# Moving constants and raw weight tiles to the lower end of SBUF, and six weight units to the upper end, in a two-layer hybrid decoder trunk

## The chip, the cores and the metric

The kernel runs on one core of a Trainium2 chip. The metric is the device time of one execution in microseconds (us). One execution was also profiled; its trace is what the views below are taken from.

## The reference

Input x is (1, 1024, 1024) float32: 1024 positions, 1024 features. Two layers follow each other, each a token mixer and a dense feed-forward part, both with a residual addition and an RMS norm ahead of them; a last RMS norm closes the trunk.

```python
for layer in range(2):
    hn = rms_norm(h, norm_mix_g[layer])
    if layer % 2 == 0:
        h = h + mixer_ab(hn, ...)     # gated DeltaNet heads, short gated convolutions
    else:
        h = h + mixer_cd(hn, ...)     # HGRN2 heads, dilated sliding-window attention
    hn = rms_norm(h, norm_ffn_g[layer])
    h = h + (silu(hn @ w_gate[layer]) * (hn @ w_up[layer])) @ w_down[layer]
return rms_norm(h, norm_final_g)
```

The feed-forward width is 2816, which is 22 blocks of 128.

## The kernel before

**Numbers.** Every large product is made in float32r with both operands split into a high and a low part. `split` (L103, L104) lets ScalarE copy the float32 source into the high part and VectorE subtract to get the low part. `mm3` (L127 to L129) then issues three matmuls for each block: high weights with high data, high weights with low data, low weights with high data. Each has a 128x128 stationary block (the weights) and a moving tile of 128x512; in two functions of the second mixer, `swa_v` and `hgrn_v`, the sides are exchanged: the normalised data hn is stationary and a 128x256 piece of weights moves. In all, `mm3` issues 3750 such triples.

**SBUF.** Tiles come from pools that are stacked from either end of SBUF, the lower ("left") or the upper ("right"). Three are open throughout: "hnp" at the lower end with eight quarters (8192 bytes per partition each) for the normalised data; "ring" at the upper end with four weight units `w` (8192 bytes: a high and a low half), two raw tiles (4096 bytes) into which DMAs bring weights, and a pad; and "const", below the ring, with masks, the identity, gains and a pad. All others are opened and closed stage by stage between these. A tile that takes the place of an earlier one waits for that tile's last users.

**Weights.** For every product the SP queue loads a raw tile from DRAM (L116 in the mixers, L267 in the gate and up projections, L518 in the down projection), and the splits turn it into a unit. TensorE waits for a unit's two halves only.

**Gate and up projections (class `Up`).** For each f of the 22 blocks the gate and up products are combined by a Strassen-Winograd scheme of seven half-size products on both 512-position halves at once: a11, a12, s1, s2, s3, a22 and s4, 12 matmuls each. Their moving tiles are quarters: two of the norm (hn in the trace), t1 and b22 in hnp, t2, t3 and t4 in the pool "hx". Four weight units are filled for each f, by four calls of `part`: part_a (a11 and a12), part_b (s2 and s1), part_c (s3 and a22), part_d (s4). GpSimd makes the sums that b, c and d need. `part` counts its calls, and from the ninth on, two of every six take a unit in the pool "up" (tags w0 and w1), the other four one of the ring:

```python
self.n += 1
i = self.n - 9
u = self.right.tile([P, 2, DM], F32R, tag=f"w{i % 6}", name="w", bufs=1) if i >= 0 and i % 6 < 2 else unit()
```

From f = 3 on this puts parts c and d on w0 and w1 where f is a multiple of 3, parts a and b where f leaves 2, and none where f leaves 1. Together with part d of f = 1 and part b of f = 2, 576 matmuls of each layer have their weights there. The pool "up" lies directly below const and also holds four tiles `hid` for results on their way to DRAM and four tiles `kr` for kept partial sums. In `end`, the a22 and s4 products of one f close its two results, which VectorE (L370) and GpSimd (L378) multiply and the SP queue stores.

**Down projection (`down`).** Products over all 22 blocks, with the hidden values loaded back from DRAM, split into hidq tiles, and weights through raw tiles and ring units. Before the results are added to the residual (L537), h is loaded back from DRAM (L168) into tiles of the pool "trunk", which take the place of what "up" held.

**Order.** The start of `Up` (`turn`) is issued in the written order on TensorE, VectorE, ScalarE and GpSimd; elsewhere a scheduler orders each engine's instructions when the program is built.

Addresses in the program as built, in bytes within a partition:

| tiles | before | after |
|---|---|---|
| const | 183296 to 188288 | 16512 to 21504 |
| raw (two) | 221056 to 229248 | 21504 to 29696 |
| hn quarters (hnp) | 16512 + 8192 n | 29696 + 8192 n |
| t2, t3, t4 (hx) | 82048 + 8192 n | 95232 + 8192 n |
| w0, w1 (up) | 150528, 175104 | 180096, 188288 |
| four ring units | 188288 + 8192 n | 196480 + 8192 n |
| hid (four) | 158720 to 166912 | 163712 to 171904 |
| kr (four) | 166912 to 175104 | 171904 to 180096 |

Of the kernel before, what the change touches and what calls it, by code (L numbers as in the profile page):

```python
# [9 lines left out]
F32 = mybir.dt.float32  # L10
# [8 lines left out]
P = 128  # L19
T_LEN = 1024  # L20
DM = 1024
# [31 lines left out]
def hybrid_trunk_kernel(ctx: ExitStack, tc: tile.TileContext, x_t, w_all, w_four, w_down, w_ba, vecs, c_f, c_i, c_rope, out):  # L53
# [4 lines left out]
    def pool(name, side="left", space=None):  # L58
        kw = {} if space is None else {"space": space}
        if space is None:  # L60
            kw["side"] = side
        if space is not DRAM:
            kw["reuse_waits"] = "tile"
        return tc.tile_pool(name=name, bufs=1, **kw)

    hnp = ctx.enter_context(pool("hnp"))
    ring = ctx.enter_context(pool("ring", side="right"))
    const = ctx.enter_context(pool("const", side="right"))
    ps = ctx.enter_context(pool("ps", space=PSUM))
    dr = ctx.enter_context(pool("dr", space=DRAM))  # L70

# [19 lines left out]
    def psg():  # L91
        return ps.tile([P, HT], F32, tag="g", name="psg", bufs=2)
# [4 lines left out]
    def psm():  # L97
        return ps.tile([P, HT], F32, tag="m", name="psm", bufs=3)


    def split(hi, lo, src, eng=V):

        S.copy(hi, src)  # L103
        eng.tensor_tensor(lo, src, hi.bitcast(F32), op=SUB)  # L104

    def unit():

        return ring.tile([P, 2, DM], F32R, tag="w", name="w", bufs=4)

    def wload(*names):  # L110

        us = []
        for n in names:
            us.append(unit())
            raw = ring.tile([P, DM], F32, tag="raw", name="raw", bufs=2)
            dma(raw, w_all[W_AT[n]])  # L116
            split(us[-1][:, 0, :], us[-1][:, 1, :], raw)
        return us
# [21 lines left out]
    def quarter(pool_=None, name="hn"):  # L140

        p, n = (hnp, 8) if pool_ is None else (pool_, 6)
        return tuple(p.tile([P, KH, HT], F32R, tag="hn", name=name + "hl"[z], bufs=n) for z in range(2))
# [109 lines left out]
    class Up:  # L253
# [9 lines left out]

        def raw(self, kind, f, spare=False):
            t = self.left.tile([P, DM], F32, tag="spare", name="raw", bufs=1) if spare else \
                ring.tile([P, DM], F32, tag="raw", name="raw", bufs=2)
            dma(t, w_all[W_AT[kind, self.layer, f]])  # L267
            return t

# [77 lines left out]
        def kept(self, left, name):  # L347
            if left:
                return self.snaps.tile([P, HT], F32, tag="kl", name=name, bufs=2)
            return self.right.tile([P, HT], F32, tag="kr", name=name, bufs=4)  # L350

        def p6(self, f, t2):
# [54 lines left out]
        def turn(self, tr, row, b11, b21, hx, close, left, right):  # L407

            for f in range(2):
                self.part_a(f, self.raw("g", f))  # L410
            u0 = self.raw("u", 0, True)
            self.part_a(2, self.raw("g", 2))
            g0 = self.raw("g", 0)
            s = self.sums(g0, u0)
            G.tensor_tensor(u0[:, :HT], g0[:, :HT], u0[:, :HT], op=SUB)
            G.tensor_tensor(g0[:, HT:], g0[:, HT:], s[:, :HT], op=SUB)
            low = self.prepared(0, s, "s2", "s1")
            self.p1(0, b11)
            dg = tr.rms(1, between=low)
            self.p2(0, b21, psg())  # L420
            pb = tr.spread(dg)
            self.p1(1, b11)
            self.p2(1, b21, psg())
            self.p1(2, b11)
            self.p2(2, b21, psm())
            tr.short.close()
            self.snaps = left("snaps")

            (a0, b0), (a1, b1) = tr.h[0], tr.h[1]
            lo, hi = slice(0, 2), slice(2, 4)  # L430
            t1, b22 = quarter(name="t1"), quarter(name="b22")
            t2, t3, t4 = quarter(hx, "t2"), quarter(hx, "t3"), quarter(hx, "t4")
            self.t12 = t1, t2

            def comb(dst, x, y, c):
                V.tensor_tensor(dst[:, c, :], x[:, c, :], y[:, c, :], op=SUB)

            def high(t, src):
                for c in (lo, hi):
                    S.copy(t[0][:, c, :], src[:, c, :])  # L440

            def rest(t, src):
                for c in (lo, hi):
                    V.tensor_tensor(t[1][:, c, :], src[:, c, :], t[0][:, c, :].bitcast(F32), op=SUB)

            tr.scale(1, row, pb, (0,))
            self.part(0, u0, "s3", "a22")
            g1 = self.snap(0)
            u1 = self.raw("u", 1)
            tr.scale(1, row, pb, (1, 2, 3))  # L450
            comb(a0, a1, a0, lo)
            comb(a0, a1, a0, hi)
            high(t1, a0)
            s = self.left.tile([P, DM], F32, tag="s", name="ws", bufs=1)
            G.tensor_tensor(s[:, HT:], u1[:, :HT], u1[:, HT:], op=ADD)
            w1 = self.raw("g", 1, True)
            tr.scale(1, row, pb, range(KH, KT))
            rest(t1, a0)
            low_d = self.prepared(0, g0, None, "s4")
            self.p5(0, t1, psm())  # L460
            V.tensor_tensor(s[:, :HT], s[:, HT:], w1[:, :HT], op=SUB)
            low = self.prepared(1, s, "s2", "s1")
            comb(a0, b1, a0, lo)
            low()
            self.p5(1, t1, psm())
            comb(a0, b1, a0, hi)
            high(t2, a0)
            rest(t2, a0)
            g2 = self.snap(1)
            comb(a1, b1, a1, lo)  # L470
            comb(a1, b1, a1, hi)
            high(t3, a1)
            self.p6(0, t2)
            self.p6(1, t2)
            self.add11(0, g1)
            self.add11(1, g2)
            rest(t3, a1)
            V.tensor_tensor(u1[:, :HT], w1[:, :HT], u1[:, :HT], op=SUB)
            low = self.prepared(1, u1, "s3", "a22")
            comb(b0, b0, a0, lo)  # L480
            low()
            comb(b0, b0, a0, hi)
            high(t4, b0)
            low_d()
            u2 = self.raw("u", 2)
            rest(t4, b0)
            high(b22, b1)
            V.tensor_tensor(w1[:, HT:], w1[:, HT:], s[:, :HT], op=SUB)  # L488
            rest(b22, b1)
            close()  # L490
            self.right = right("up")
            self.part(1, w1, None, "s4")
            self.first = [self.hidden()]
            w2 = self.raw("g", 2)
            self.loads = 1
            s = self.sums(w2, u2)
            self.p7(0, t3)
            self.p7(1, t3)
            self.part_b(2, s)
            self.end(0, t4, b22)  # L500
            self.end(1, t4, b22)
            self.c11(2)
            self.p5(2, t1, psg())
            self.p6(2, t2)
            self.part_c(2, w2, u2)
            self.part_d(2, w2, s)
            return b22, t3, t4

    def down(layer, hid, tr, hx, hr, src, step, after):
# [4 lines left out]

        def weights(src, n):
            w = unit()
            raw = ring.tile([P, DM], F32, tag="raw", name="raw", bufs=2)
            dma(raw[:, 0:n], src)  # L518
            split(w[:, 0, 0:n], w[:, 1, 0:n], raw[:, 0:n])
            return w  # L520

        def operand(half, i):

            p, b = (hx, 6) if next(kinds) == "x" else (hnp, 8)
            q = slots[half, i] = p.tile([P, KH, HT], F32R, tag="hn", name="hidq", bufs=b)
            raw = hr.tile([P, 2, HT], F32, tag="hr", name="hr", bufs=2)
            dma(raw, hid[half, 2 * i:2 * i + 2].rearrange("f p t -> p f t"))
            split(q[:, 0:2, :], q[:, 2:4, :], raw)
# [57 lines left out]
    def out_proj(name, cat_d, tr, src, order, half, hp):  # L586
        qs = {}
        for k in order:
            if k // KH not in qs:
                qs[k // KH] = quarter()  # L590
            f = hp.tile([P, HT], F32, tag="m", name="cin", bufs=4 - layer)
            dma(f, cat_d[k])
            split(hk(qs, 0, k), hk(qs, 1, k), f)
        tr.begin(half, src)
        for d0 in range(0, KT, 2):
            w = wload((name, d0), (name, d0 + 1))
            for i in range(2):
                o = proj(wk(w, i), qs, order, psg() if i else psu())
                h = tr.at(half, d0 + i)
                V.tensor_tensor(h, h, o, op=ADD)  # L600
                tr.piece(half, d0 + i)
                tr.save(half, d0 + i, hd[2 * layer][half])
                yield
# [1051 lines left out]
```

## Time and profile before

| what | value |
|---|---|
| median of 3 runs | 2769.38 us (2766.91 to 2775.9) |
| the profiled execution | 2768.24 us, its span 2766.5 us |
| mean granted TensorE clock | 0.994 |
| TensorE busy | 98% of the span, 15180 matmuls |
| VectorE, ScalarE, GpSimd busy | 53%, 36%, 17% |
| DMA | 312.83 MB, mean 113 GB/s |

The span runs from the first to the last instruction; the profiled execution's own time has a little around it. Matmuls are pipelined: one starts before the one before it has ended, so what counts for TensorE is the interval from start to start, and the durations in the trace (about 390 ns) are longer than that. The gate and up projections take about 592 to 989 us and 2116 to 2514 us of the span, the down projections what follows, to 1260 us or so and to the end.

### The profile page before, as it was taken

Reading aid. Unit: us, or ns where it says so; the run is one execution under the profiler, and the core shown is the slowest. Engines: PE = TensorE matmul, PEld = TensorE weight load, DVE = VectorE, ACT = ScalarE, POOL = GpSimd, SP = SyncE. Lnnn points to the kernel's source line nnn. Section 1 sums busy time; section 2 is a strip of 40 time slices with the busy share of each in tenths; the row PEclk is TensorE's granted clock in tenths of the full one; section 3 lists DMA queues with packets and bytes.
Section 4 is the critical chain, followed back from the end, with each engine's and each line's share of the span. In section 5 each row is a group of like instructions: output and inputs, shape, how many; then the busy total and the mean of one; then the engine's idle time right before and its main releaser. Section 6 shows DMA issues by size and latency. Waiting matters only on the chain. (4 is left out here: it accounts for less than half of the span.)

```text
span 2766.5 us, 38080 instructions
## 1 busy us (share of the span) xinstructions
PE 2708.2 (98%) x15180; PEld 2240.8 (81%) x15180; DVE 1469.7 (53%) x2469; ACT 989.7 (36%) x1671; POOL 476.2 (17%) x436
## 2 busy tenths in 40 slices
PE   8999999989999999999999999999998999999998
PEld 6777788867888888889888897887886788887887
DVE  7777666563434443444655756556557433335333
ACT  4422123343333342323444434444434333334231
POOL 0100111334333201010000000000033333330100
PEclk9999999999999999999999999999999999999999
DMA  4324346522222274442132221333652222227343
GB/s 148 120 90 157 95 128 195 183 73 88 80 80 84 91 264 137 137 127 77 47 89 85 66 85 47 88 86 88 217 164 76 85 81 84 84 88 266 100 137 107
DMA packets 165954, 312.83 MB, mean 113 GB/s; under 512 B 22256, under 2 KB 71696, under 8 KB 164624
## 3 DMA queue, kind: packets, MB, share of 16 engines
q1 hardware_dynamic: 165776, 310.40, 35.7%
q8 instruction: 119, 1.95, 0.3%
q14 instruction: 59, 0.48, 0.1%
HBM read 236.32 MB, written 74.01 MB: 112 GB/s over the span
## 5 line engine op out<-in xcount | busy, mean ns | idle before, releaser
L104 DVE TENSOR_TENSOR w<-raw,w 128x1024 fp32r<-128x1024 f32 (+2 forms) x332 | 408.2, 1231 | 608.2 <-ACT w L103 607.5
L103 ACT CAST w<-raw 128x1024 fp32r<-128x1024 f32 (+2 forms) x332 | 327.1, 986 | 664.9 <-PE psm L129 233.8
L127 PE MATMUL psu<-hnh,w 128*128 128x512 f32 x1328 | 531.0, 400 | 7.0 <-ACT w L103 7.0
L129 PE MATMUL psu<-hnh,w 128*128 128x512 f32 x1328 | 524.5, 395 | 0.0
L128 PE MATMUL psu<-hnl,w 128*128 128x512 f32 x1328 | 523.5, 395 | 0.0
L127 PEld LDWEIGHTS psu<-hnh,w 128*128 128x128 f32 x1328 | 250.6, 189 | 57.0 <-ACT w L103 7.3
L129 PEld LDWEIGHTS psu<-hnh,w 128*128 128x128 f32 x1328 | 250.0, 188 | 51.8 <-DVE w L104 1.0
L128 PEld LDWEIGHTS psu<-hnl,w 128*128 128x128 f32 x1328 | 250.7, 189 | 49.2 <-DVE hnl L1491 0.2
L187 POOL TENSOR_TENSOR acc<-acc,sq 128x512 f32<-128x512 f32 x48 | 73.3, 1528 | 503.3 <-ACT sq L183 400.2
L127 PE MATMUL psu<-w,hnh 128*128 128x256 f32 x512 | 149.9, 293 | 0.0
L129 PE MATMUL psu<-w,hnl 128*128 128x256 f32 x512 | 145.7, 284 | 0.0
L128 PE MATMUL psu<-w,hnh 128*128 128x256 f32 x512 | 145.3, 284 | 0.0
L127 PE MATMUL psu<-hidq,w 128*128 128x512 f32 (+1 forms) x352 | 134.8, 383 | 0.0
L129 PE MATMUL psu<-hidq,w 128*128 128x512 f32 (+1 forms) x352 | 134.6, 382 | 0.0
L128 PE MATMUL psu<-hidq,w 128*128 128x512 f32 (+1 forms) x352 | 134.6, 382 | 0.0
L302 POOL TENSOR_TENSOR raw<-raw,ws 128x512 f32<-128x512 f32 x40 | 55.7, 1393 | 326.4 <-DVE w L104 326.4
L378 POOL TENSOR_TENSOR hid<-gt,c 128x512 f32<-128x512 f32 x44 | 78.4, 1781 | 138.3 <-ACT gt L376 119.1
L127 PEld LDWEIGHTS psu<-w,hnh 128*128 128x128 f32 x512 | 98.5, 192 | 0.6
L128 PEld LDWEIGHTS psu<-w,hnh 128*128 128x128 f32 x512 | 98.7, 193 | 0.1
L129 PEld LDWEIGHTS psu<-w,hnl 128*128 128x128 f32 x512 | 98.4, 192 | 0.0
L1161 POOL COPY attn<-ac 32x128 f32<-32x128 f32 x32 | 13.4, 420 | 435.0 <-DVE ac L1158 392.4
L287 POOL TENSOR_TENSOR ws<-raw 128x512 f32<-128x512 f32 x42 | 63.1, 1502 | 123.5 <-DVE raw L488 65.1
(398 smaller groups left out, 5671.6 us busy)
## 6 DMA issues: line engine op xcount, KB each, us to landing
raw<-in_dram SPq DMA_DIRECT2D x282, 512.0 KB, 3.7
hid<-hid SPq DMA_DIRECT2D x88, 256.0 KB, 2.1
hr<-hid SPq DMA_DIRECT2D x44, 512.0 KB, 4.5
hd<-h SPq DMA_DIRECT2D x48, 256.0 KB, 4.2
h<-hd SPq DMA_DIRECT2D x48, 256.0 KB, 5.5
scr_c<-cx SPq DMA_DIRECT2D x8, 1216.0 KB, 4.6
cxb<-scr_c SPq DMA_DIRECT2D x8, 1216.0 KB, 5.9
h<-in_dram SPq DMA_DIRECT2D x32, 256.0 KB, 5.1
```

What stands on the lines that cost most here:

```text
L103: S.copy(hi, src)
L104: eng.tensor_tensor(lo, src, hi.bitcast(F32), op=SUB)
L127: T.matmul(o, lh, rh, start=first and i == 0, stop=False, **kw)
L128: T.matmul(o, lh, rl, start=False, stop=False, **kw)
L129: T.matmul(o, ll, rh, start=False, stop=last and i == n - 1, **kw)
L187: (eng or G).tensor_tensor(a, a, q, op=ADD)
L287: G.tensor_tensor(s[:, HT:], b[:, :HT], b[:, HT:], op=ADD)
L302: G.tensor_tensor(a[:, HT:], a[:, HT:], s[:, :HT], op=SUB)
L378: G.tensor_tensor(h, g, self.c22.pop(f), op=MULT)
L1161: G.tensor_copy(attn[z, :, z], ac[z])
```

## The change

The pool "const" is opened first, at the lower end, so that hnp and all that is stacked on it lie 13184 bytes higher. The raw tiles become tiles of const; the ring keeps its four units and its pad. In `turn`, one tile hid and one tile kr are taken ahead of the first unit w0, so that the pool "up" has its four hid and four kr tiles below and w0 and w1 at its upper end, next to the ring. On every engine the instructions and their order are the same as before; addresses change, and with them some of the waits of tiles that take the place of others.

```diff
+    const = ctx.enter_context(pool("const"))
     hnp = ctx.enter_context(pool("hnp"))
     ring = ctx.enter_context(pool("ring", side="right"))
-    const = ctx.enter_context(pool("const", side="right"))
...
-            raw = ring.tile([P, DM], F32, tag="raw", name="raw", bufs=2)
+            raw = const.tile([P, DM], F32, tag="raw", name="raw", bufs=2)
...
-                ring.tile([P, DM], F32, tag="raw", name="raw", bufs=2)
+                const.tile([P, DM], F32, tag="raw", name="raw", bufs=2)
...
         def kept(self, left, name):
             if left:
                 return self.snaps.tile([P, HT], F32, tag="kl", name=name, bufs=2)
+            if self.first_kept:
+                return self.first_kept.pop()
             return self.right.tile([P, HT], F32, tag="kr", name=name, bufs=4)
...
             self.right = right("up")
+            self.first, self.first_kept = [self.hidden()], []
+            self.first_kept.append(self.kept(False, "c22"))
             self.part(1, w1, None, "s4")
-            self.first = [self.hidden()]
```

The first hunk for raw stands in `wload`, the second in `Up.raw`; `weights` in `down` has the same edit.

More of the change, by code (lines that the diff above doesn't have):

```diff
@@ L516, in weights @@
             w = unit()
-            raw = ring.tile([P, DM], F32, tag="raw", name="raw", bufs=2)
+            raw = const.tile([P, DM], F32, tag="raw", name="raw", bufs=2)
             dma(raw[:, 0:n], src)
```

## The prediction

> **What bounds the kernel now.** I read the page first: span and busy times, then who TensorE waits for, then single matmuls in the timeline.
>
> ```profile
> span 2766.5 us, 38080 instructions
> ...
> PE 2708.2 (98%) x15180; PEld 2240.8 (81%) x15180; DVE 1469.7 (53%) x2469; ACT 989.7 (36%) x1671; POOL 476.2 (17%) x436
> ```
>
> TensorE is busy for 2708.2 of 2766.5 us, so all its idle time is 58.3 us. Its three longest waits, in the view of waits for PE:
>
> ```profile
> PE psu L127 <- ACT w L103: 10.2, 3, 7.0
> PE psu L127 <- ACT c L360: 7.8, 4, 3.2
> PE psu L127 <- ACT gt L333: 6.3, 4, 3.0
> ```
>
> No wait is worth more than 10.2 us. What can move this kernel by a per cent is the interval at which matmuls start, and it isn't one number. The timeline of TensorE (start, duration, name) shows the a22 and s4 products of f = 6 in the first feed-forward stage, a22 with its weights in unit w0 of the "up" pool and s4 in w1:
>
> ```profile
> 693.55 0.40 PE L127 MATMUL psu<-t4h,w 128*128 128x512 f32 x1
> 693.79 0.40 PE L128 MATMUL psu<-t4l,w 128*128 128x512 f32 x1
> ...
> 698.67 0.40 PE L128 MATMUL psg<-b22l,w 128*128 128x512 f32 x1
> 698.90 0.40 PE L129 MATMUL psg<-b22h,w 128*128 128x512 f32 x1
> ```
>
> One f later the same two products, with both weights in units of the ring:
>
> ```profile
> 713.15 0.39 PE L127 MATMUL psu<-t4h,w 128*128 128x512 f32 x1
> 713.38 0.39 PE L128 MATMUL psu<-t4l,w 128*128 128x512 f32 x1
> ...
> 718.14 0.39 PE L128 MATMUL psg<-b22l,w 128*128 128x512 f32 x1
> 718.37 0.40 PE L129 MATMUL psg<-b22h,w 128*128 128x512 f32 x1
> ```
>
> Both stretches are 24 matmuls on the same moving tiles, t4 and b22. The first takes 698.90 - 693.55 = 5.35 us for 23 intervals, 232.6 ns each; the second 718.37 - 713.15 = 5.22 us, 227.0 ns each. TensorE has no gap in either, and the granted clock is 1.00 in both. Laying the program's order of matmuls beside the trace's start times gives every interval its weight tile. Without intervals over 260 ns, 1124 intervals on w0 and w1 have a mean of 232.8 ns, and 7888 on the four ring units 227.6 ns (226 or 227 for most). Only the address of the weights differs: w0 and w1 start at 150528 and 175104, multiples of 1024; ring units start at 188288 + 8192 n, 896 above a multiple of 1024. All moving tiles (hn, t1 to t4, b22, hidq) start 128 above a multiple of 2048.
>
> It isn't the neighbours' work either: where ScalarE, VectorE and GpSimd are all idle, the means are 233.3 ns and 227.0 ns. Nor is a low address slow in itself. In swa_v and hgrn_v the hn tiles are the weights (addresses 16512 to 82048) and ring units the moving side:
>
> ```profile
> 1490.04 0.28 PE L129 MATMUL psu<-w,hnl 128*128 128x256 f32 x1
> ...
> 1491.12 0.28 PE L129 MATMUL psu<-w,hnl 128*128 128x256 f32 x1
> ```
>
> Nine intervals in 1.08 us, 120.0 ns each: half of 226.7 ns is 113.3, so 6.7 ns more than half, steady, as on the ring.
>
> **The change part by part.** *Instructions.* None is added, removed or moved: each engine has the same sequence in both programs. That costs 0.
>
> *Waits.* A few change owner. The loads of h in `down` (L168) wait for hid's stores, not for matmuls, or the other way round; the first eight are issued at 995.0 us, after the last hid store at 994.08 us, and the queue issued other loads between, so at most the landing of that store (2.1 us, the page's median for hid) could be added per layer. Queued behind the loads on SP are the next raw and hr loads, for which units of TensorE's coming products wait. h itself is read only at the additions of L537, after the first 264 matmuls of the stage, and TensorE is busy for 250.00 of the 250 us from 1010 us on, so this is hidden: 0, and 2 x 2.1 us if the cover were gone. The first hid of the second layer (L378, GpSimd) loses two of three waits; the one that ends last there is for ScalarE's gt and stays: 0.
>
> *Addresses, what the change is.* w0 and w1 move to 180096 and 188288, the ring to 196480 and above: all six units are now 896 above a multiple of 1024. hnp, hx and all else on the left moves up by 13184 bytes, so every moving tile moves from 128 to 0 above a multiple of 1024. Two readings of the trace part here.
>
> Reading 1: the weights' own address decides. All six units then sit as the ring did, and 1152 matmuls gain 232.8 - 227.6 = 5.2 ns: -6.0 us.
>
> Reading 2: the distance between weights and moving tile decides. Modulo 512 the ring's distance is 384 - 128 = 256, and in the 256-wide matmuls, with the sides exchanged, 128 - 384 is 256 too: both steady. For w0 and w1 it is 0 - 128 = 384: slow. In the changed program it is 384 - 0 = 384 for all six units. Then w0 and w1 stay slow and the ring becomes slow. (Modulo 1024 or 2048 the distances also fall on those of w0 and w1; a longer period would show in the slow stretches as a step every three matmuls, where the weights advance by 512 bytes and the moving row by 2048, and they show none.)
>
> I take reading 2. In both stretches the load of the next weights starts 2 to 4 ns after a matmul and lasts 188 ns (median); what grows is the time to the next matmul's start, with both streams under way. A distance is what two streams have; a weight tile that is slow because it is aligned to 1024, by itself, is the stranger story. The rows can't exclude it: no row has another moving offset.
>
> The sum by reading 2, step by step:
> - 512-wide matmuls: 3750 triples (L127 to L129) are 11250; 1536 of the rows "psu<-w,hnh" and "psu<-w,hnl" and 132 in `last` are 256 wide, which leaves 9582. Less 1152 on w0 and w1: 8430 x 5.2 ns = +43.8 us.
> - 256-wide: 1668 matmuls. Bounds 0 (they stay at 120) and 5.2 ns each (the nearest slow row), 0 to +8.7 us; sides exchanged, their distance becomes 0 - 384 = 128, which no row has. I take the middle, +4.3 us.
> - Waits that a slower TensorE fills: L127's wait for w and those like it. Bounds 0 and -10.2 us (the longest cause); most of its 10.2 us is one wait of 7.0 us at the start, before any matmul, so I take -3 us.
> - float32 matmuls of the mixers: their tiles all shift by the same 13184 bytes except ident and the masks in cf; 0, within 1 us.
>
> Sum +45.1 us. The profiled execution took 2768.24 us (its span and 1.7 us around it); the median of the runs shown is 2769.38, 1.1 us more. 2768.24 + 45.1 = 2813.3; against the median 2814.5. I say 2814.
>
> The Trainium skill, page "TensorE: Matmul & The Clock Gate", section "Step-by-step: what each phase is for", speaks against both readings: "Loading the next tile's weights doesn't steal SBUF read bandwidth from the running matmul." By that rule no address could change an interval, and the sum would be 0. The trace doesn't agree with it as a rule for this kernel: 232.6 against 227.0 ns on the same moving tiles.
>
> **The rivals.** *Faster: reading 1.* -6.0 us as above; if the ring's intervals in the two feed-forward stages also settle from 228.0 to the 226.8 of `down` (2140 x 1.2 ns = 2.6 us, some of it a tail after each change from w0 or w1), -8.6 us: 2761 to 2763. For it: every ring interval is steady, and the new units have the ring's offset. Against it: the moving tiles move too. It decides as soon as the moving tile's offset is without effect; no size of any other cost matters.
>
> *A boundary in address.* Weights at or above about 188000 are fast, those below 183296 slow. Then the unit at 188288 becomes fast and the one at 180096 stays slow: half of 6.0 us, 2766. Against it stand the 120.0 ns of hn weights at 16512 to 82048.
>
> *No change.* Loading takes nothing from the matmul, and the 5 ns belong to something else in the parts on w0 and w1, such as the moment at which they are made, which the change leaves alone: 2769. Against it: the means of w0 and w1 are the same in both layers (232.6 and 233.1 ns each time), over seven kinds of products made at different moments.
>
> *Reading 2 in part.* Only products on hn and hidq, or only the first matmul of a triple, become slow: 2780 to 2800.
>
> **How the numbers follow.** 0.3% of the median, 8.3 us, is about what a measurement of this kernel can tell from no change; -6.0 us lies within it and -8.6 us just beyond. Reading 2 in full: 0.52, at 2814; with 256-wide matmuls from 0 to 5.2 ns, filled waits from 0 to 10.2 us and 0.3 ns either way on the 5.2, 2800 to 2824. Reading 2 in part: 0.07. Reading 1: 0.29, of which 0.15 with the settling beyond 8.3 us and 0.14 without. Boundary 0.05, no effect 0.07. So slower 0.59, same 0.26, faster 0.15. A range that holds 8 in 10 has to reach from reading 1 to reading 2: 2760 to 2824; that of the likeliest case alone is 2800 to 2824.
>
> **What would show it.** In the profile after: a stretch like 713.15 to 718.37 at 5.35 us, no longer 5.22, and the same in `down`, where 1010 to 1260 us of before has a mean of 226.8 ns throughout; PE's busy time up by some 45 us with its count of 15180; waits of TensorE no longer than now. Reading 1 shows instead 227 ns on all six units in the feed-forward stages and nothing changed in `down`. If intervals stay as they are and the time still moves by 10 us or more, the working above is wrong as a whole: then a wait has appeared, in the waits for PE, and the likeliest place is the start of `down`.

## The result and the profile after

| | before | after |
|---|---|---|
| median, both run on one chip | 2769.86 us (6 runs, 2762.3 to 2775.9) | 2797.97 us (6 runs, 2796.12 to 2801.54) |
| profiled execution, its span | 2768.24 us, 2766.5 us | 2796.12 us, 2794.4 us |

The ratio is 1.0101, with a 95% interval of 1.0089 to 1.0112: the change costs 28 us. The forecast was slower, 2814 us, so the sign and the cause were foreseen and the size was too large by 16 us; the time lies in the wide range (2760 to 2824) and 2 us below that of the likeliest case (2800 to 2824).

The head of the page after:

```profile
span 2794.4 us, 38079 instructions
...
PE 2741.8 (98%) x15180; PEld 2243.7 (80%) x15180; DVE 1470.6 (53%) x2469; ACT 989.1 (35%) x1671; POOL 476.7 (17%) x436
```

TensorE has the same 15180 matmuls and is busy 33.6 us longer; its idle time went from 58.3 to 52.6 us. The other engines' busy times moved by 1 us at most. Its waits, three largest:

```profile
PE psu L127 <- ACT w L103: 10.5, 3, 7.2
PE psu L127 <- ACT gt L333: 6.6, 4, 2.5
PE psu L127 <- ACT c L362: 6.2, 4, 3.2
```

No wait appeared or grew with more than 0.3 us. (L362 is the L360 of before, two lines lower.) So the time lies in the matmuls. The timeline of the a22 and s4 products for f = 6 (weights in w0 and w1) and f = 7 (ring):

```profile
697.46 0.39 PE L127 MATMUL psu<-t4h,w 128*128 128x512 f32 x1
...
702.80 0.39 PE L129 MATMUL psg<-b22h,w 128*128 128x512 f32 x1
...
717.08 0.39 PE L127 MATMUL psu<-t4h,w 128*128 128x512 f32 x1
...
722.42 0.39 PE L129 MATMUL psg<-b22h,w 128*128 128x512 f32 x1
```

702.80 - 697.46 = 5.34 us and 722.42 - 717.08 = 5.34 us: before, the first took 5.35 and the second 5.22. The stretch on w0 and w1 stayed slow, the one on the ring became slow. In `down` the same shows in the view of windows, as the number of TensorE's instructions in 190 us without a gap, first of before, then of after:

```profile
1010.00:1200.00 190.00, 190.00 (x852) 157.75 (x851) 72.42 (x75) 60.38 (x70) 17.26 (x11) 1.00 0.48 152
```

```profile
1010.00:1200.00 190.00, 190.00 (x832) 154.58 (x831) 70.55 (x72) 58.35 (x67) 17.23 (x11) 1.00 0.49 159
```

Twenty fewer, with the granted clock (the third number from the end) at 1.00 in both; the mean interval of the float32r matmuls there went from 227.0 to 232.6 ns. The 256-wide matmuls, with the sides exchanged:

```profile
1505.06 0.28 PE L129 MATMUL psu<-w,hnl 128*128 128x256 f32 x1
...
1506.13 0.28 PE L129 MATMUL psu<-w,hnl 128*128 128x256 f32 x1
```

Nine intervals in 1.07 us, 118.9 ns; they had been 120.0. These became slightly faster, which the prediction did not foresee.

Since the order of matmuls is the same, the two traces can be laid beside each other interval by interval. An interval is put to the weights of the matmul that ends it. A "stop" is here an interval of 260 ns or more in either trace, whatever held TensorE up.

| intervals | count | before, us | after, us | difference, us |
|---|---|---|---|---|
| 512 wide, ring, short in both | 7854 | 1788.06 | 1825.93 | +37.9 |
| 512 wide, w0 and w1, short in both | 1126 | 261.94 | 262.00 | +0.1 |
| 256 wide, short in both | 1600 | 196.95 | 195.90 | -1.1 |
| float32 and between kinds, short in both | | | | -0.9 |
| stops | | | | -8.6 |

The sum is +27.4 us from the first matmul to the last; the span grew by 27.9.

### The profile page after: what moved, and what is told of

The parts are those of the page before. It is cut to its first block, busy times and chain, and to the rows that moved or that the text cites. A ratio compares the mean times of both kernels' runs of the same rounds, so it can differ in the third digit from the quotient of the medians.

```text
span 2794.4 us, 38079 instructions
## 1 busy us (share of the span) xinstructions
PE 2741.8 (98%) x15180; PEld 2243.7 (80%) x15180; DVE 1470.6 (53%) x2469; ACT 989.1 (35%) x1671; POOL 476.7 (17%) x436
## 4 chain that ended last, share of the span: by engine, by line
PE 88%; DVE 4%; DMA 3%; ACT 3%; issue 1%; POOL 1%; SPq 0%; POOLq 0%; DVEq 0%; ACTq 0%
PE psu L127 19%; PE psu L129 18%; PE psu L128 18%; PE psg L129 5%; PE psg L127 5%; PE psg L128 5%; PE psm L127 3%; PE psm L128 3%; PE psm L129 3%; DMA raw<-in_dram 1%; PE psm L1304 1%; PE psm L1321 1%; DMA cxb<-scr_c 1%; DVE cacc L760 1%; DVE w L104 1%
## 5 line engine op out<-in xcount | busy, mean ns | idle before, releaser
L103 ACT CAST w<-raw 128x1024 fp32r<-128x1024 f32 (+2 forms) x332 | 326.4, 984 | 687.9 <-PE psm L129 239.7
L127 PE MATMUL psu<-hnh,w 128*128 128x512 f32 x1328 | 536.0, 404 | 7.2 <-ACT w L103 7.2
L128 PE MATMUL psu<-hnl,w 128*128 128x512 f32 x1328 | 529.5, 399 | 0.0
L127 PEld LDWEIGHTS psu<-hnh,w 128*128 128x128 f32 x1328 | 251.5, 189 | 61.3 <-ACT w L103 7.2
L127 PE MATMUL psu<-w,hnh 128*128 128x256 f32 x512 | 149.4, 292 | 0.0
L127 PE MATMUL psu<-hidq,w 128*128 128x512 f32 (+1 forms) x352 | 136.6, 388 | 0.0
L127 PEld LDWEIGHTS psu<-w,hnh 128*128 128x128 f32 x512 | 97.3, 190 | 0.6
```

The source lines that it names most:

```text
L127: T.matmul(o, lh, rh, start=first and i == 0, stop=False, **kw)
L128: T.matmul(o, lh, rl, start=False, stop=False, **kw)
```

## The experiments

Each was run beside the kernel before on the same chip, and each ratio is to that. The two kernels of trains leave the trunk out; the others compute all of it.

**Single matmuls, by distance.** A kernel of its own with trains of 24 matmuls one after the other (56 trains, not 64 as the expectation says). Per train the byte offsets of weights and moving tile differ; eight trains are 256 wide, eight are in bfloat16 and four, of 12 matmuls, in float32:

```python
mms += [(wh, mh), (wh, ml), (wl, mh)]          # four k, twice; 128x128 weights, 512-wide moving
...
T.matmul(o[:, 0:width], w[:, a:a + 128], m[:, b:b + width], start=i == 0, stop=i == len(mms) - 1)
```

> This kernel leaves the whole trunk out: it only runs 64 trains of matmuls with other engines idle, each train with the address pattern of one triple loop and with one distance from the moving tiles to the weights (weights minus moving, modulo 512). Tiles of the two sides start 128 above a multiple of 512; a train then shifts one side or both. Theory D (the distance decides): float32r trains of width 512 have 226.7 ns from start to start at distance 256 and 232 to 233 ns at 384; a shift of both sides by the same 64, 128 or 256 bytes changes nothing; whether the period is 256 or 512 is read from distances 0 and 128 (0 as 256 and 128 as 384 if it is 256). Theory W (the weights' own address decides): the intervals follow the weights' offset alone, and trains with the moving tiles shifted and the weights fixed are all alike. Theory M (the moving tiles' own offset decides): trains with the weights shifted and the moving tiles fixed are all alike. If D holds, some distance that is no multiple of 128 may be faster than 226.7 ns or slower than 233. Width 256: 120 at distance 256, 118 to 120 elsewhere. bfloat16 and float32 trains: no theory says.

Measured, mean of the last 18 intervals of a train, in ns:

| distance weights - moving, mod 512 | 0 | 32 | 64 | 96 | 128 | 160 | 192 | 224 |
|---|---|---|---|---|---|---|---|---|
| float32r, 512 wide | 226.7 | 233.3 | 233.3 | 234.1 | 232.7 to 233.3 | 233.3 | 228.9 | 233.3 |
| the same, distance + 256 | 226.7 | 233.3 | 233.3 | 234.1 | 232.7 to 233.3 | 233.3 | 228.9 | 233.2 |
| float32r, 256 wide | 120.0 | | 117.8 | | 118.4 | | 117.8 | |

The timeline joins a train into one row; its columns are start, duration, and at the end the count of matmuls. The train at distance 256, then the one at 384:

```profile
55.42 5.38 PE L60 MATMUL o<-mov_r,wts_r 128*128 128x512 f32 x23
```

```profile
77.68 5.29 PE L60 MATMUL o<-mov_r,wts_r 128*128 128x512 f32 x22
```

The 23 matmuls of the first row make 22 intervals, the 22 of the second 21. Less the last matmul's own 0.39 us: (5.38 - 0.39) / 22 = 226.8 ns, and (5.29 - 0.39) / 21 = 233.3 ns. No other engine and no DMA was at work in those stretches, and the granted clock was 1.00:

```profile
50.00:85.00 35.00, 35.00 (x152) 28.28 (x152) 0.00 (x0) 0.00 (x0) 0.00 (x0) 1.00 0.00 0
```

Shifting both streams together by 64, 128 or 256 bytes kept each distance's value (226.7 to 228.1 ns at 0 and 256, 232.0 to 232.7 at 128 and 384); shifting the moving side alone, with the weights left where they were, gave 228.9, 232.5, 233.3 and 226.7 ns at distances 448, 384, 320 and 256. So the distance decides at all offsets tried, with a period of 256 bytes, and no address by itself. With bfloat16 every distance tried (0 to 224 in steps of 32) gave 215.8 ns, with float32 (0 to 192 in steps of 64) 429.2 ns for a record of the trace. The first train began with intervals of 426 and 427 ns, nearly double, ahead of the trace's first record of the clock, and is left out; distance 0 was run again later.

**The change with its distance repaired.** The changed kernel without the two pads, so that all six units and all moving tiles start 480 above a multiple of 512, distance 0:

```diff
-    const.tile([P, 8], F32, name="pad")
...
-    ring.tile([P, 24], F32, name="pad")
```

> The changed kernel without its two pads (32 bytes in const, 96 in the ring): the moving tiles go down by 32 bytes and the weight units up by 96, so that both stand 480 above a multiple of 512 and the distance is 0. Theory D with period 256: all six units at 226.7 to 228 ns, about 2762 us, 35 us faster than the changed kernel and 6 to 9 us faster than the kernel before. Theory D with period 512: another value than at 256 or 384, unknown between them. Theory W or M: nothing says that 480 is slow or fast; the ring's 384 and hn's 128 were the fast values, so under W the ring could stay fast and under M hn could stay slow.

Measured: 2767.31 us median (2763.17 to 2770.38), ratio to before 0.9983 (0.9974 to 0.9992). The same products of f = 6 in its timeline (all lines one lower):

```profile
697.11 0.39 PE L126 MATMUL psu<-t4h,w 128*128 128x512 f32 x1
...
702.33 0.39 PE L128 MATMUL psg<-b22h,w 128*128 128x512 f32 x1
```

5.22 us. The expectation of about 2762 us was 5 us too low: laid beside before, short intervals on w0 and w1 gave 5.2 us, but stops took 5.9 back. The whole rest of the change is in this kernel, and all 28 us are gone: const and raw at the lower end, the moved waits at L168 and L378, and the six units side by side cost nothing that this measurement can tell.

**The kernel before with w0 and w1 moved by 128 bytes.** Only they change distance, from 128 to 0 modulo 256:

```diff
             self.part_b(2, s)
+            self.right.tile([P, 32], F32, name="pad")
```

> The kernel before with a tile of 128 bytes more at the upper end of the pool up, which puts w0 and w1 128 bytes lower, at distance 256 like the ring; nothing else of the change. Theories D and W: the 1152 matmuls on w0 and w1 go from 232.6 to 227 ns, -6.0 us, with the tails in the ring up to -8.6 us: 2761 to 2764 us. Theory of a boundary in address (units above 188000 are fast): nothing changes, 2769 us. Theory M: nothing changes, as the moving tiles stay.

Measured: 2765.79 us median (2763.21 to 2773.28), ratio 0.9985 (0.9976 to 0.9993). Their stretch of f = 6:

```profile
692.95 0.39 PE L127 MATMUL psu<-t4h,w 128*128 128x512 f32 x1
...
698.16 0.39 PE L129 MATMUL psg<-b22h,w 128*128 128x512 f32 x1
```

5.21 us instead of 5.35. The expectation was 2761 to 2764 us. The short intervals on w0 and w1 gave 5.1 us, the ring's 0.6; stops took 2.7 us back. A little of that shows in the waits for PE, for ScalarE's gt: 6.7 us where before had 6.3.

```profile
PE psu L127 <- ACT gt L333: 6.7, 4, 2.8
```

This kernel and the one without pads are below the kernel before by 0.15% and 0.17%; between the two there is no telling.

**The loss without the change.** The kernel before with 64 bytes less of pad in the ring. The moving tiles stay where they were; the ring with raw, const and the pool "up" lie 64 bytes higher, at the same end as before. Ring distance 64 instead of 0, w0 and w1 192 instead of 128:

```diff
-    ring.tile([P, 24], F32, name="pad")
+    ring.tile([P, 8], F32, name="pad")
```

> The kernel before with the ring's pad cut from 24 to 8 floats and nothing else: const, raw and all moving tiles stay where they were; the ring units, const and the pool up lie 64 bytes higher. Distance modulo 256: ring 64 instead of 0, w0 and w1 192 instead of 128. Theory distance (scan: 233.3 ns at 64, 228.9 ns at 192): the ring's 7854 short intervals go from 227.6 to 232.5 or 233.3 ns, +38 to +45 us; w0 and w1 gain 2.5 to 3.6 ns on 1126, -3 to -4 us; waits fill by some 5 us; 2798 to 2808 us without any part of the change. Rival, the loss needs the other parts of the change (const and raw at the lower end, moving tiles on multiples of 1024): 2770 us.

Measured: 2801.96 us median (2797.64 to 2803.11), ratio 1.0111 (1.0098 to 1.0125). Laid beside before: 7872 short intervals on the ring +44.6 us (to 233.3 ns), w0 and w1 -2.4 us, 256 wide -4.1 us. Products of f = 7 in its timeline:

```profile
721.63 0.39 PE L127 MATMUL psu<-t4h,w 128*128 128x512 f32 x1
...
726.99 0.39 PE L129 MATMUL psg<-b22h,w 128*128 128x512 f32 x1
```

5.36 us, 233.0 ns each. No part of the change is needed for the loss; 64 bytes of padding do it.

**The change without its last part.** The changed kernel with hid and kr taken where they were before, so that w0 and w1 lie at 163712 and 188288, apart but still at distance 128:

```diff
-            if self.first_kept:
-                return self.first_kept.pop()
...
-            self.first, self.first_kept = [self.hidden()], []
-            self.first_kept.append(self.kept(False, "c22"))
             self.part(1, w1, None, "s4")
+            self.first = [self.hidden()]
```

> The changed kernel without its last part: hid and kr are not taken ahead of the first unit, so w0 and w1 stay apart in the pool up (at 163712 and 188288); const and raw stay at the lower end. Distance of all six units is still 128 modulo 256. Theory distance: 2798 us as in the changed kernel, w0 and w1 at 232.5 ns as before. Rival, the six units side by side cost something by themselves: 2785 to 2795 us.

Measured: 2799.94 us median (2797.43 to 2802.41), ratio 1.0104 (1.0088 to 1.0119). The interval overlaps the changed kernel's; taken with the kernel without pads, which has the units side by side and loses nothing, it shows no effect of the six units' being neighbours.

**A distance between.** The changed kernel with the ring's pad cut from 24 to 8 floats, distance 192 for all six units:

```diff
-    ring.tile([P, 24], F32, name="pad")
+    ring.tile([P, 8], F32, name="pad")
```

> The changed kernel with the ring's pad cut from 24 to 8 floats, so that all six weight units lie 64 bytes higher: their distance to the moving tiles becomes 192 modulo 256 instead of 128, and nothing else moves. Theory distance: the scan gave 228.9 ns at 192, 233 ns at 128 and 226.7 ns at 0. About 9000 short 512-wide intervals were 232.5 ns in the changed kernel and 227.5 to 228.7 ns with distance 0 (2767 us); at 192 they should lie between, 228.9 to 230 ns: 2772 to 2782 us, some 18 to 25 us below the changed kernel. Rival, only distance 0 counts in the whole kernel, everything else costs the same: 2798 us as in the changed kernel.

Measured: 2768.83 us median (2766.73 to 2772.52), ratio 0.9995 (0.9987 to 1.0004). This missed the 2772 to 2782 expected, on the good side. The 512-wide intervals came as expected, 229.2 ns, and cost 14.0 us against the kernel without pads. But the 256-wide ones, left out of that expectation, fell to a median of 114 ns and gave back 7.5 us:

```profile
1488.33 0.28 PE L129 MATMUL psu<-w,hnl 128*128 128x256 f32 x1
...
1489.35 0.28 PE L129 MATMUL psu<-w,hnl 128*128 128x256 f32 x1
```

Nine intervals in 1.02 us, 113.3 ns. With the sides exchanged, their distance in this kernel is 64. The trains had shown 117.8 ns for 256 wide at the distances 64 and 192; the trunk's 256-wide matmuls have other steps between their tiles, and what of that makes the 4 ns is open.

**How fine, and whose weights.** Trains again, with offsets for even and odd matmuls given apart:

> The trunk is left out again; 23 trains of 24 float32r matmuls, 512 wide, one after the other without other work. Offsets are given for the even and the odd matmuls of a train, relative to equal starts modulo 512. Question 1: which weights count, the matmul's own or those that are loaded for the next one while it streams? Theory N (next load): the interval after a matmul depends on the offset of the NEXT matmul's weights less the offset of the moving tile that is streaming. Moving (0, 128) with weights (0, 128): every next load stands 128 from the running stream, so 233 ns throughout; moving (0, 128) with weights (128, 0): distance 0 each time, 227 ns throughout. With moving (0, 0) and weights (0, 128) the intervals alternate, slow after even matmuls and fast after odd ones, mean about 230 ns. Rival O (own weights): the first is 227 ns, the second 233 ns. Question 2: how fine is it? If only distance 0 modulo 256 is fast, the trains at 4, 8, 12, 16, 24, 240 and 252 bytes show 233 ns and 256 shows 226.7; if there is a granule below 32 bytes, the smallest distances are still at 226.7.

Measured: 232.2 ns at 4 bytes, 230.7 at 8, 230.0 at 12 (alternating 224 and 236) and at 24, 233.3 at 16, 32 and 64; 226.7 at 240, 252 and 256, 232.2 at 260. The expectation that 240 and 252 are slow was wrong: the fast place reaches at least 16 bytes below a multiple of 256 and not 4 above it. The rows of 252 and 260:

```profile
71.78 5.60 PE L55 MATMUL o<-mov_r,wts_r 128*128 128x512 f32 x24
```

```profile
82.67 5.51 PE L55 MATMUL o<-mov_r,wts_r 128*128 128x512 f32 x23
```

(5.60 - 0.39) / 23 = 226.5 ns and (5.51 - 0.39) / 22 = 232.7 ns. The distances 8, 12 and 24, expected at 233 or 227 ns, lie between. On whose weights count, neither theory held: moving (0, 128) with weights (0, 128) gave 228.3 ns where the next-load theory said 233 and the own-weights theory 227; with weights (128, 0) 230.0 ns throughout, where they said 227 and 233. With moving (0, 0) and weights (0, 128), where slow and fast intervals in turn with a mean of about 230 were expected, the mean was 232.2 ns: 233.6 after even matmuls and 230.9 after odd ones, so none were fast. The two other mixed trains gave 230.2 and 230.3. What the two streams do to each other inside an interval stays open; that their distance sets the interval does not hang on it.

## Why the prediction was right in sign and too large

By its own steps:

- *Instructions, 0*: right, 15180 matmuls in both.
- *Waits at L168 and L378, 0*: right; the kernel without pads has the same changed waits and is at 0.9983.
- *Reading 2*: right, and shown four ways: by trains without any other work, by repairing the distance in the changed kernel, by repairing it for w0 and w1 alone, and by spoiling it in the kernel before. Reading 1 and the boundary fall with the trains: weights left in place became slow and fast as the moving tile alone was shifted. "No change" falls with the 5.34 us on the ring. "Reading 2 in part" falls too: in the profile after, the means for the seven kinds of moving tile, on the ring and on w0 and w1, lie between 232.0 and 233.6 ns, and those for the first, second and third matmul of a triple between 232.4 and 232.9. The period is 256, not 512; for the 512-wide matmuls of this case that makes no difference.
- *512-wide, forecast +43.8, measured +37.9.* Two factors were too large. The price was 232.8 - 227.6 = 5.2 ns; paired intervals give 232.5 - 227.7 = 4.8. And 8430 counted every matmul of the products, though those at stops and at the border to other kinds of work do not have the short interval: 7854 do.
- *256-wide, forecast +4.3, measured -1.1.* The step that failed in sign. It had no row for distance 128 with the sides exchanged and set its lower bound at 0 because 120.0 ns looked like the settled value. The trains show that for 256 wide 120.0 ns, at distance 0, is the slowest of the four distances tried. A gain should have stood in the bounds.
- *Waits filled, forecast -3, measured -8.6* (all stops together). Within its bounds of 0 to -10.2, near the far end. The granted clock has little part in it: 512-wide intervals of 425 to 428 ns, several in a row, number 37 before and 38 after. The wait that the term named, L127's for w at L103, was not filled (10.2 and 10.5 us); c at L360 was (7.8 to 6.2), and vch at L761 (3.3 to 1.7, there at L764). How much of the 8.6 us belongs to the change is open: each figure is from one execution, and in the changed kernel without its last part and in the one with 64 bytes less, both as slow, stops lost only 2.6 and 3.3 us against the same trace of before, which is what was forecast.
- *float32, 0 within 1 us*: -0.9 with the borders between kinds.

The surplus of 45.1 over 27.4 us is made of 5.9 + 5.4 + 5.6 + 0.9, less 0.1 on w0 and w1: three terms of about the same size, all leaning one way. The range of the likeliest case, 2800 to 2824, missed the median by 2 us. Its lower end has the price near what was measured (4.9 ns) and the waits at their far bound, but still counts 8430 intervals, which at 4.9 ns is 2.8 us more than 7854 of them, and allows the 256-wide ones no gain, which is 1.1 us.

The rule weighed in the prediction, from the Trainium skill, page "TensorE: Matmul & The Clock Gate", section "Step-by-step: what each phase is for", that loading the next tile's weights takes no read bandwidth from the running matmul, would have made the change free. The Trainium skill's page "SBUF — State Buffer", section "Who interferes with whom", says likewise that only the port pair shared by VectorE and GpSimd causes contention. For float32r the runs don't agree with either: the interval is 226.7 or 233.3 ns by the distance of the two operands, with nothing but TensorE at work. For bfloat16 and float32 the runs show nothing against them at the distances tried.

## What to carry to other kernels

Where TensorE is busy 98% of the time, read single intervals from the timeline before looking for waits: two stretches of the same matmuls that differ by 2% are a term of the sum. For float32r with 512-wide moving tiles, work out the address of the weights less that of the moving tile, modulo 256, whenever pools are rearranged; a pad of some tens of bytes can be worth 1%, as the 64 bytes here. A cost taken from two groups' means should be counted only on the intervals that have those means, and an operation without a row needs a bound below nothing too.

## What was not expected of the hardware

- The interval of a 512-wide float32r matmul depends on the distance of its two operands (weights less moving) modulo 256 bytes: 226.7 ns at 0, 252 and 240, 228.9 at 192, about 230 at 8, 12 and 24, 232 to 234 at the others tried. For 256 wide, 0 is the slowest of the distances tried: 120.0 ns, against 117.8 at 64 in the trains and 113.3 at 64 in the trunk. With bfloat16 (215.8 ns) and float32 (429.2 ns) no such effect showed.
- The slow intervals are no fixed number: within a train they wander between 228 and 241 ns at distance 128, and alternate 224 and 236 at 12, while at distance 0 they settle at 226 or 227, in some trains only after a few intervals of up to 236.
